# Buffers of their own for the S5 gate's sigmoid tiles, and explicit waits for each mixed piece, in a hybrid trunk kernel

## The chip, the cores and the metric

The kernel runs as one launch on one core of a Trainium2 chip. The metric is the device time of that launch in microseconds (us); lower is better. The median of three runs of the kernel before is 1204.6 us (1203.15 to 1209.52). About 0.5%, 6 us, is what a measurement can tell from no change.

## What is computed

One layer of a hybrid decoder trunk on 1024 positions of width 1024, in float32. The normalized input goes through one wide projection, whose columns feed three branches: an RG-LRU recurrence (512 wide), a gated delta rule with 8 heads of 128 (chunks of the sequence with a state carried from one to the next), and an S5 state space model (512 wide) with a gate. The three outputs stand side by side (2048 wide), are multiplied by the output weights, added to x, and a gated embedding and a last norm follow. The reference, cut to the two branches that matter here and what follows them:

```python
def step(state, inp):                      # gated delta rule, one chunk
    q_i, k_i, u_i, w_i, aqk_i, gc_i = inp
    v_new = u_i - jnp.einsum('bhcd,bhde->bhce', w_i, state)
    o_i = jnp.einsum('bhcd,bhde->bhce', q_i * jnp.exp(gc_i)[..., None], state) + jnp.einsum('bhij,bhje->bhie', aqk_i, v_new)
    state = state * jnp.exp(g_last)[..., None, None] + jnp.einsum('bhcd,bhce->bhde', k_dec, v_new)
...
z5 = jax.nn.gelu(y_s5)                     # S5 with its gate
y_s5 = z5 * jax.nn.sigmoid(z5 @ s5_w_glu[i].astype(f32) + s5_b_glu[i].astype(f32))
y_s5 = y_s5 * jax.nn.silu(s5_gate.astype(f32))
mix = jnp.concatenate([y_rg.astype(dt), y_gdn.astype(dt), y_s5.astype(dt)], axis=-1)
h = h + mix @ w_out[i]
```

## The kernel before

**How the order of the work is made.** The whole program is one Python class, `Trunk`. Its parts are generators (tasks); `spawn` (L214) registers one, a `yield` names the engine on which its next instructions are due ("pe", "v" for DVE, "a" for ACT, "g" for POOL, "d" for a DMA issue on SP), and `tick` (L248) runs those whose predecessors are done and for which there is room by a small cost model (`price`, L97; the priorities stand in `PRIO`, L57). So instructions are recorded in an order that the model decides, and `pin` (L73) holds every engine to that order. Matmuls that nothing holds up go out through `fill` (L200), which calls `tick` after every few of them: these are the filler between which the tasks' own matmuls and transposes (`mm` L195, `tr` L198) are placed. `need` (L269) keeps recording until named tasks are done.

**Precision.** Every large product is three matmuls of 128x512 in a split of float32 into a high and a low part: high times high, high times low, low times high. ACT makes the high part (a cast), DVE or POOL the low part (a subtraction).

**Stages.** A short projection of the embedding stands first; then the wide projection in 48 blocks (tiles hhi, hlo by whi, wlo into pp) is the filler for the RG-LRU, the S5 part and the heads. For each head, `k_post` multiplies the key tile kT by itself (two tiles of four 128x128 products in PSUM, 8 matmuls), DVE turns these into AT (L1130), `solve` inverts triangular blocks on DVE for two heads at once, `levels` puts the inverses together on PE, and `chain` (L1285 and after) walks 8 steps. A step of the chain is a loop through two engines: PE Sm by kT and qT (into pc, po), DVE R (L1292), PE R by XT, DVE V (L1304), PE V by kd and AQ, DVE the new Sm (L1316) and the output on (L1327). `finish` (L1345 to L1354) scales on, transposes it on PE, and stores the head to DRAM as a piece of `mix`. All heads' chains follow each other; head 7's is the last.

**The S5 gate, `glu`.** Four blocks of 128 columns; each has two halves, and each half is 12 matmuls (gzh, gzl by whi, wlo into pp), so 96 matmuls in all. ACT takes the sigmoid of a half into the tile gs (L1432), `pre` loads gz and gg and POOL multiplies them (L1412), DVE multiplies gs by the result (L1416), SP stores gs as piece 12 + i of mix (L1418). These 96 matmuls are the filler beside the chain of head 7.

**The output projection, `out_proj`.** Four groups (two halves of the columns by two halves of the rows), each over 16 pieces of mix in the order 0 to 10, 12 to 15, 11 (11 is head 7). A piece is a load from DRAM (mr, by `mstream`, L1514 to L1522), a cast on ACT and a subtraction on DVE (mhl, L1506, L1508), and 12 matmuls, so 192 a group; at most three pieces are in hand. The weights (wsr, ws) go through ACT and POOL, by `wstream`. Group 0 accumulates in the two pp and two pg buffers; pp is also what the gate's halves use.

**Slots.** SBUF is nearly full, so tiles of late stages live in slots of earlier ones (L38): kT has four, kd one, dec two, AT three, sz two, cy one. Before the change a gate tile takes slot kT for blocks 0 and 2 and slot kd for 1 and 3, so `glu` has two waits:

```python
self.need(*t[-2:-1])      # the block before the last one must be stored
if i:
    self.need(last)       # head 6 must be finished
```

`k_post` takes both of its product tiles from the pool psg, which has two buffers; the pool psa has two more.

Of the kernel before, what the change touches and what calls it, by code (L numbers as in the profile page):

```python
# [12 lines left out]
F32 = mybir.dt.float32  # L13
# [9 lines left out]
P = 128  # L23
# [5 lines left out]
HEADS = 8  # L29
# [17 lines left out]
class Trunk:  # L47
# [1051 lines left out]
    def k_post(self, h, cv):  # L1099
        nc, d = self.nc, self.hd[h]  # L1100
        kT = d["kT"]
        hs = slice(h * NT, (h + 1) * NT)
        dec = yield from self.load_dec(h)
        ss = self.tiny.tile([P, NT], F32, name="kss", bufs=2)
        AT = d["AT"] = self.slot("AT", [P, NT, P], "AT")
        yield "pe", lambda: cv[1].done and cv[1].ready <= self.now and self.room(self.psg, 2)
        pts = [self.ps(self.psg, [P, 4, P], 8) for _ in range(2)]
        for q, pt in enumerate(pts):
            if q:
                yield "pe"  # L1110
            self.products(pt, kT, kT, q)
            yield "v"
            for k in range(4):
                t = 4 * q + k
                nc.vector.scalar_tensor_tensor(out=AT[:, t, :], in0=pt[:, k, :], scalar=1.0, in1=self.ident,
                                               op0=ALU.mult, op1=ALU.mult, accum_out=ss[:, t:t + 1])
                if k == 1:
                    yield
        nc.vector.tensor_scalar(out=ss, in0=ss, scalar1=EPS, scalar2=None, op0=ALU.add)
        r = yield from self.rsqrt(self.tiny, ss, NT, "kr")  # L1120
        bp = d["bp"] = self.tiny.tile([P, NT], F32, name="bp", bufs=5)
        nc.vector.tensor_tensor(out=bp, in0=r, in1=r, op=ALU.mult)
        nc.vector.tensor_tensor(out=bp, in0=bp, in1=self.beta[:, hs], op=ALU.mult)
        sk = d["sk"] = self.tiny.tile([P, NT], F32, name="sk", bufs=5)
        nc.vector.tensor_tensor(out=sk, in0=ss, in1=r, op=ALU.mult)
        for q, pt in enumerate(pts):
            yield "v"
            for k in range(4):
                t = 4 * q + k
                nc.vector.scalar_tensor_tensor(out=AT[:, t, :], in0=pt[:, k, :], scalar=bp[:, t:t + 1],  # L1130
                                               in1=dec[:, t, :], op0=ALU.mult, op1=ALU.mult)
                if k == 1:
                    yield
        self.decs -= 1
        yield "d"
        for b in range(4):
            bs = slice(32 * b, 32 * b + 32)
            nc.sync.dma_start(out=self.adiag[h, b].rearrange("t j i -> j t i"), in_=AT[bs, :, bs])
# [261 lines left out]
            self.decs -= 1  # L1400
            zs.append((hi, lo))

    def glu(self, zs, bg):
        nc = self.nc

        def pre(i, box):
            z = self.slot("cy", [P, S], "gz")
            nc.sync.dma_start(out=z, in_=self.zd[i])
            g = self.slot("sz", [P, S], "gg")
            nc.sync.dma_start(out=g, in_=self.sgd[i])  # L1410
            yield "g"
            nc.gpsimd.tensor_tensor(out=g, in0=g, in1=z, op=ALU.mult)  # L1412
            box.append(g)

        def glu_post(i, sig, box):
            nc.vector.tensor_tensor(out=sig, in0=sig, in1=box[0].rearrange("p (j c) -> p c j", c=P), op=ALU.mult)  # L1416
            yield "d"
            nc.sync.dma_start(out=self.mix[12 + i], in_=sig.rearrange("p c j -> p (c j)"))  # L1418
        t, last = [], self.hd[HEADS - 2]["fin"]
        for i in range(4):  # L1420
            wh, wl = self.take(("g", i))
            self.need(*t[-2:-1])
            if i:
                self.need(last)
            sig = self.slot("kd" if i % 2 else "kT", [P, P, 8], "gs")
            box = []
            pr = self.spawn(pre(i, box), "d", t[-1:] + [last])
            for half in range(2):
                sl = slice(512 * half, 512 * half + 512)
                ps = self.psum()  # L1430
                self.mm3(ps, [((wh[:, k, :], wl[:, k, :]), (zs[k][0][:, sl], zs[k][1][:, sl])) for k in range(4)])
                self.drains.append(self.spawn(self.drain(ps, lambda ps, half, sl, i=i, sig=sig: nc.scalar.activation(  # L1432
                    out=sig[:, :, 4 * half:4 * half + 4].rearrange("p c j -> p j c"),
                    in_=ps.rearrange("p (j c) -> p j c", c=P), func=AF.Sigmoid, bias=bg[:, i:i + 1]), half), "a", self.drains[-1:]))
            t.append(self.spawn(glu_post(i, sig, box), "v", self.drains[-1:] + [pr]))
        return t
# [74 lines left out]
    def mstream(self):  # L1511
        nc = self.nc
        n = 0
        for nh in range(2):  # L1514
            for g in range(2):
                for k in self.korder:
                    yield "d", lambda: self.mused + 3 > n and n < len(self.ms) + 2 and (k != 4 + HEADS - 1 or self.hd[HEADS - 1]["fin"].done)
                    raw = self.slot("dec", [P, 512], "mr")
                    nc.sync.dma_start(out=raw, in_=self.mix[k, :, 512 * g:512 * g + 512])
                    m = self.slot("AT", [P, 2, 512], "mhl", F32R)  # L1520
                    self.spawn(self.split_late(raw, m, (nh, g, k), self.ms, nc.vector), "a", prio=self.PRIO["split_soon"])
                    n += 1  # L1522

    def until(self, store, key):
        self.wait(lambda: key in store)
        return store[key]
# [61 lines left out]
        self.hT[t] = (th, tlo)  # L1588

    def stream_setup(self):  # L1590
        self.ws, self.ms, self.wused, self.mused = {}, {}, 0, 0
        self.norms, self.hT, self.hs = {}, {}, {}
        self.korder = list(range(3 + HEADS)) + [12, 13, 14, 15, 3 + HEADS]

# [68 lines left out]
    def build(self):  # L1663
        tc, nc = self.tc, self.nc
        with ExitStack() as st:
# [4 lines left out]
            cp = E(tc.tile_pool(name="const", bufs=1))  # L1670
# [23 lines left out]
            with ExitStack() as s5s:  # L1694
# [17 lines left out]
                for kind, i in ORDER:  # L1712
# [11 lines left out]
                    elif kind == "x":  # L1724
                        last = rg[1:]
                        t, gate = self.rg_tile(i, rg)
# [13 lines left out]
            with tc.tile_pool(name="gdn", bufs=1) as self.gp:  # L1740
                hd = self.hd
                bg = self.load(cp, "s5_b_glu", [P, 4])
                hd[0]["solve"] = hd[1]["solve"] = self.spawn(self.solve(0), "d", [hd[0]["k"], hd[1]["k"]])
                hd[0]["levels"] = self.spawn(self.levels(0), "g", [hd[0]["solve"]])
                self.q_proj(0)
                self.v_proj(0)
                self.z_proj(0)
                zs = []
                prep = self.gdn(zs)
                hst.close()  # L1750
                self.fr = st.enter_context(tc.tile_pool(name="fr", bufs=1, side="right"))
                self.stream_setup()
                self.spawn(self.wstream(), "d", [prep])
                self.spawn(self.mstream(), "d", [prep])
                self.need(prep)
                self.glu(zs, bg)
                self.out_proj()
                self.ple(cp)


def layout(x, norm_g, w_in, rg_lambda, gdn_a_log, gdn_dt_bias, **kw):
# [38 lines left out]


def program(shapes):
    nc = bacc.Bacc("TRN2", target_bir_lowering=False, num_devices=1, dynamic_dma_scratch_size=8192)
    ins = {n: nc.dram_tensor("in_" + n, s, F32, kind="ExternalInput").ap() for n, s in shapes.items()}
    out = nc.dram_tensor("out_y", (S, D), F32, kind="ExternalOutput").ap()
    with tile.TileContext(nc) as tc:
        Trunk(tc, ins, out).build()
    nc.compile()
    return nc
# [7 lines left out]
```

## Time and profile before

| what | value |
|---|---|
| median of three runs (lowest, highest) | 1204.6 us (1203.15, 1209.52) |
| the profiled execution, its time | 1201.29 us |
| its span, first to last instruction | 1199.6 us |
| mean granted TensorE clock | 0.968 |
| PE busy | 1111.2 us (93% of the span) |
| DVE, ACT, POOL busy | 776.5, 566.2, 159.6 us (65%, 47%, 13%) |
| all DMA queues | 140.18 MB, mean 117 GB/s |

PE is the engine with the most work, and the table says how much: 88 us of the span have no matmul. An idle microsecond on PE is worth one on the end only if nothing else sets the time there, and the granted clock tells a second loss: a matmul that takes 0.40 us at the full clock takes 0.63 us when the clock is granted at half. The profiled execution is 3.3 us under the median of the runs.

### The profile page before, as it was taken

The numbers are of one execution on the slowest core, as the hardware profiler recorded it, in microseconds if no ns is written. First come the engines' busy times: TensorE is split into PE (matmuls) and PEld (weight loads), VectorE is DVE, ScalarE is ACT, GpSimd is POOL, SyncE is SP. The second block draws the span as 40 slices with busy tenths as digits, with TensorE's granted clock in tenths as the row PEclk, the third lists the DMA queues.
The fourth block names the chain that finished last, engine by engine and source line by source line (L and its number), as shares of the span: only waits on it lengthen the run. The fifth ranks groups of instructions, "written<-read, shape, count | busy, mean of one in ns | idle before, by whom it ended". The sixth has DMA issues, their size and how long they took to land. (4 is left out here: it accounts for less than half of the span.)

```text
span 1199.6 us, 17257 instructions
## 1 busy us (share of the span) xinstructions
PE 1111.2 (93%) x6165; PEld 902.7 (75%) x6165; DVE 776.5 (65%) x1933; ACT 566.2 (47%) x1138; POOL 159.6 (13%) x166
## 2 busy tenths in 40 slices
PE   6899698999979998999999999999868999999996
PEld 4576477887867776788888888878656778878885
DVE  6877586965676775886688667865744243263665
ACT  6533546745667773344534454435641243243332
POOL 1100000000001010000000000000261042044442
PEclk9999799999989999799999999999989999999999
DMA  8311345474766331212121122122454465464222
GB/s 302 114 36 44 105 126 174 109 190 101 214 198 189 101 114 32 73 47 80 54 84 53 36 93 67 53 53 81 148 187 166 129 212 175 135 202 147 71 85 92
DMA packets 85222, 140.18 MB, mean 117 GB/s; under 512 B 31760, under 2 KB 42192, under 8 KB 85136
## 3 DMA queue, kind: packets, MB, share of 16 engines
q1 hardware_dynamic: 83984, 134.88, 36.5%
q0 software_dynamic: 1152, 4.19, 0.9%
q8 instruction: 49, 0.80, 0.3%
q14 instruction: 37, 0.30, 0.1%
HBM read 97.98 MB, written 31.49 MB: 108 GB/s over the span
## 5 line engine op out<-in xcount | busy, mean ns | idle before, releaser
L195 PE MATMUL pp<-hhi,whi 128*128 128x512 f32 x768 | 315.9, 411 | 4.5 <-ACT hhi L404 2.3
L195 PE MATMUL pp<-hlo,whi 128*128 128x512 f32 x768 | 313.1, 408 | 3.1 <-DVE hlo L407 3.1
L195 PE MATMUL pp<-hhi,wlo 128*128 128x512 f32 x768 | 314.1, 409 | 1.3 <-DVE wlo L425 1.3
L195 PEld LDWEIGHTS pp<-hhi,whi 128*128 128x128 f32 x768 | 147.0, 191 | 35.6 <-ACT hhi L404 3.3
L195 PEld LDWEIGHTS pp<-hlo,whi 128*128 128x128 f32 x768 | 146.6, 191 | 33.1 <-DVE hlo L407 4.0
L195 PEld LDWEIGHTS pp<-hhi,wlo 128*128 128x128 f32 x768 | 146.5, 191 | 30.3 <-issue 2.4
L477 DVE SCALAR_TENSOR_TENSOR cy<-raw,c_gdn_conv_w,cy 128x512 f32<-128x512 f32 x144 | 108.2, 751 | 15.2 <-ACT cy L473 12.3
L1508 DVE TENSOR_TENSOR mhl<-mr,mhl 128x512 fp32r<-128x512 f32 x64 | 54.6, 854 | 88.4 <-ACT mhl L1506 88.4
L195 PE MATMUL pg<-ws,mhl 128*128 128x512 f32 x384 | 101.2, 398 | 0.5 <-ACT mhl L1506 0.5
L1508 POOL TENSOR_TENSOR ws<-wsr,ws 128x512 fp32r<-128x512 f32 x48 | 68.0, 1421 | 196.9 <-ACT ws L1506 196.7
L425 DVE TENSOR_TENSOR wlo<-wraw,whi 128x1024 fp32r<-128x1024 f32 (+1 forms) x52 | 63.1, 1214 | 40.5 <-ACT whi L423 36.9
L195 PEld LDWEIGHTS pg<-ws,mhl 128*128 128x128 f32 x384 | 71.3, 188 | 19.5 <-ACT mhl L1506 1.5
L1506 ACT CAST mhl<-mr 128x512 fp32r<-128x512 f32 x64 | 39.8, 622 | 93.5 <-DMA mr<-mix 45.0
L195 PE MATMUL pp<-ws,fth 128*128 128x512 f32 x256 | 81.3, 396 | 0.0
L487 ACT COPY raw<-pp 128x512 f32<-128x512 f32 x56 | 32.7, 584 | 84.5 <-PE pp L195 80.2
L423 ACT CAST whi<-wraw 128x1024 fp32r<-128x1024 f32 (+1 forms) x52 | 52.8, 1015 | 24.8 <-DMA wraw<-in_w_blk 24.7
L195 PEld LDWEIGHTS pp<-ws,fth 128*128 128x128 f32 x256 | 48.0, 188 | 10.9
L1330 ACT ACTIVATE osq<-on 128x128 f32<-128x128 f32 x64 | 19.7, 308 | 75.8 <-DVE on L1327 57.9
L195 PE MATMUL pp<-ws,mhl 128*128 128x512 f32 x192 | 51.2, 399 | 3.1 <-ACT mhl L1506 1.6
L1506 ACT CAST ws<-wsr 128x512 fp32r<-128x512 f32 x48 | 29.8, 622 | 47.7 <-DMA wsr<-in_w_out 28.3
L195 PE MATMUL pp<-ws,ftl 128*128 128x512 f32 x128 | 51.1, 400 | 0.0
L1304 DVE TENSOR_SCALAR V<-pc,bp 128x128 f32<-128x128 f32 x64 | 22.3, 348 | 38.1 <-PE pc L195 38.0
(414 smaller groups left out, 2033.2 us busy)
## 6 DMA issues: line engine op xcount, KB each, us to landing
wraw<-in_w_blk SPq DMA_DIRECT2D x48, 512.0 KB, 4.2
mr<-mix SPq DMA_DIRECT2D x64, 256.0 KB, 3.0
dec<-dec SPq DMA_DIRECT2D x16, 512.0 KB, 4.5
wsr<-in_w_out SPq DMA_DIRECT2D x32, 256.0 KB, 3.0
xt<-in_xT SPq DMA_DIRECT2D x16, 256.0 KB, 6.1
ppd<-po POOLq DMA_DIRECT2D x8, 512.0 KB, 4.0
gcb<-grow SPq DMA_DIRECT2D x8, 512.0 KB, 5.0
dec<-gcb SPq DMA_DIRECT2D x8, 512.0 KB, 2.8
```

The costliest lines, as they stand in the source:

```text
L195: self.nc.tensor.matmul(**kw)
L423: nc.scalar.copy(out=hi, in_=raw)
L425: nc.vector.tensor_tensor(out=lo, in0=raw, in1=hi.bitcast(F32), op=ALU.subtract)
L477: nc.vector.scalar_tensor_tensor(out=y[:, sl], in0=raw[:, j + sl.start:j + sl.stop], scalar=wconv[:, j:j + 1], in1=y[:, sl], op0=ALU.mult, ...
L487: nc.scalar.copy(out=raw[:, 3 + 512 * half:3 + 512 * half + 512], in_=ps)
L1304: v.tensor_scalar(out=V, in0=p2, scalar1=bp[:, t:t + 1], scalar2=None, op0=ALU.mult)
L1330: nc.scalar.activation(out=sq, in_=on[:, t, :], func=AF.Square, accum_out=d["so"][:, t:t + 1])
L1506: nc.scalar.copy(out=hl[:, 0, :], in_=raw)
L1508: e.tensor_tensor(out=hl[:, 1, :], in0=raw, in1=hl[:, 0, :].bitcast(F32), op=ALU.subtract)
```

## The change

1. `k_post`: heads 0 to 2 may take their two product tiles from psa when psg has no room.
2. `glu`: the tiles gs of blocks 0 to 2 come from a pool of their own, gsig, with three buffers (128 partitions by 4 KB each); only block 3 still uses the slot kd. The wait for the block before the last is gone, and the wait for head 6 stands before block 3 alone.
3. `mstream`: a piece is loaded only when what writes it is done, for every piece (function `mixed`); before, this was written for head 7 alone, since the two waits in `glu` implied the rest.
4. The SBUF scratch that the framework sets aside for DMAs issued by POOL goes from 8192 to 4096 bytes.

```diff
@@ k_post
-        yield "pe", lambda: cv[1].done and cv[1].ready <= self.now and self.room(self.psg, 2)
-        pts = [self.ps(self.psg, [P, 4, P], 8) for _ in range(2)]
+        yield "pe", lambda: cv[1].done and cv[1].ready <= self.now and (self.room(self.psg, 2) or h < 3 and self.room(self.psa, 2))
+        pool = self.psg if self.room(self.psg, 2) else self.psa
+        pts = [self.ps(pool, [P, 4, P], 8) for _ in range(2)]
@@ glu
-        t, last = [], self.hd[HEADS - 2]["fin"]
+        t, last = self.glt, self.hd[HEADS - 2]["fin"]
         for i in range(4):
             wh, wl = self.take(("g", i))
-            self.need(*t[-2:-1])
-            if i:
+            if i == 3:
                 self.need(last)
-            sig = self.slot("kd" if i % 2 else "kT", [P, P, 8], "gs")
+            sig = self.slot("kd", [P, P, 8], "gs") if i == 3 else gs.tile([P, P, 8], F32, name="gs", bufs=3)
@@ mstream
-                    yield "d", lambda: self.mused + 3 > n and n < len(self.ms) + 2 and (k != 4 + HEADS - 1 or self.hd[HEADS - 1]["fin"].done)
+                    yield "d", lambda: self.mused + 3 > n and n < len(self.ms) + 2 and self.mixed(k)
...
+    def mixed(self, k):
+        if k < 4:
+            return True
+        if k < 4 + HEADS:
+            return self.hd[k - 4]["fin"].done
+        return len(self.glt) > k - 12 and self.glt[k - 12].done
...
+                with tc.tile_pool(name="gsig", bufs=1) as gs:
+                    self.glu(zs, bg, gs)
+                    self.out_proj()
+                    self.ple(cp)
...
-    nc = bacc.Bacc("TRN2", target_bir_lowering=False, num_devices=1, dynamic_dma_scratch_size=8192)
+    nc = bacc.Bacc("TRN2", target_bir_lowering=False, num_devices=1, dynamic_dma_scratch_size=4096)
```

Since the recorded order comes from the model, these few lines move instructions in two places. The line numbers of the changed kernel are one or more higher behind `k_post`.

**First place: PE, the key products of heads 1 and 2** (kT by kT into pg; hhi and hlo by whi are filler of the wide projection). Before:

```order
L195 MATMUL pp<-hhi,wlo 128x512
L195 MATMUL pg<-kT 128x128 x4
L195 MATMUL pp<-hhi,whi 128x512
L195 MATMUL pp<-hlo,whi 128x512
L195 MATMUL pg<-kT 128x128 x4
L195 MATMUL pp<-hhi,wlo 128x512
```

Now:

```order
L195 MATMUL pp<-hhi,wlo 128x512
L195 MATMUL pg<-kT 128x128 x8
L195 MATMUL pp<-hhi,whi 128x512
L195 MATMUL pp<-hlo,whi 128x512
L195 MATMUL pp<-hhi,wlo 128x512
```

Head 1's two tiles stand together, where two filler matmuls stood between them. Head 2's two tiles, 38 and 56 filler matmuls behind head 1's last before, now stand 32 and 45 behind; the transposes of the next task's query, 108 filler matmuls behind head 1's first tile before, stand 98 behind it.

**Second place: PE, the gate beside the chain of head 7** (gzh, gzl by whi, wlo are the gate's matmuls; pg from ident,on is the finish of head 6; pc from Sm, R, V and po are the chain). Before, from the step that follows the gate's first 24 matmuls:

```order
L195 MATMUL pc<-Sm,kT 128x128
L195 MATMUL po<-Sm,qT 128x128
L198 MATMUL pg<-ident,kT 128x128
L198 MATMUL pg<-ident,on 128x128 x4
L195 MATMUL pc<-R,XT 128x128
L195 MATMUL pc<-V,kd 128x128
L195 MATMUL po<-V,AQ 128x128
L198 MATMUL pg<-ident,on 128x128 x4
L195 MATMUL pc<-Sm,kT 128x128
```

Now, around the same finish of head 6:

```order
L195 MATMUL pp<-gzh,whi 128x512
L198 MATMUL pg<-ident,on 128x128 x4
L195 MATMUL pp<-gzl,whi 128x512
L195 MATMUL pc<-R,XT 128x128
L195 MATMUL pp<-gzh,wlo 128x512
L195 MATMUL pp<-gzh,whi 128x512
L195 MATMUL pp<-gzl,whi 128x512
L195 MATMUL pp<-gzh,wlo 128x512
L195 MATMUL pp<-gzh,whi 128x512
L195 MATMUL pc<-V,kd 128x128
L195 MATMUL po<-V,AQ 128x128
L195 MATMUL pp<-gzl,whi 128x512
```

From the first of these chain steps to the next, 8 more gate matmuls stand ahead of Sm by kT, 11 between it and the finish, 9 up to the second finish and one behind that: 29 where there was none. The gate is then through at the chain's fifth step, and the matmuls of the output projection stand between those of the later steps:

```order
L195 MATMUL pp<-gzh,wlo 128x512
L195 MATMUL pp<-ws,mhl 128x512 x3
L195 MATMUL pc<-V,kd 128x128
L195 MATMUL po<-V,AQ 128x128
L195 MATMUL pp<-ws,mhl 128x512 x3
L195 MATMUL pc<-Sm,kT 128x128
L195 MATMUL po<-Sm,qT 128x128
L198 MATMUL pg<-ident,kT 128x128
L195 MATMUL pg<-ws,mhl 128x512 x6
L195 MATMUL pc<-R,XT 128x128
```

Before, the first of them stood behind the last gate matmul, which stood 18 behind the chain's end. On DVE, the product gs of block 0 moves from behind the V of a step to ahead of it; that of block 1 stays ahead of the last step's R.

**The same place on SP** (mix from gs: store of a gate block; mr: load of a piece; gz, gg: loads for the next block; wsr: output weights). Before:

```order
L1418 DMA mix<-gs 128x1024
L1408 DMA gz<-zd 128x1024
L1410 DMA gg<-sgd 128x1024
L1519 DMA mr<-mix 128x512
L1418 DMA mix<-gs 128x1024
L1519 DMA mr<-mix 128x512
```

Now:

```order
L1419 DMA mix<-gs 128x1024
L1500 DMA wsr<-in_w_out 128x512
L1409 DMA gz<-zd 128x1024
L1411 DMA gg<-sgd 128x1024
L1519 DMA mr<-mix 128x512
L1500 DMA wsr<-in_w_out 128x512
L1519 DMA mr<-mix 128x512
L1500 DMA wsr<-in_w_out 128x512
L1519 DMA mr<-mix 128x512 x2
L1419 DMA mix<-gs 128x1024
L1519 DMA mr<-mix 128x512
```

The store at the head of the first piece is that of block 1, at the head of the second that of block 0. The fourth load of a piece, the first mr here, stood behind two stores and stands behind one; four loads stand between the first two stores where there was none, four between the second and the third, three between the third and the fourth.

## Rows read from the trace of the kernel before

**Rows 1.** Busy time in stretches: PE, PEld, DVE, ACT, POOL, then PEclk, DMA share, GB/s.

```profile
335.00:500.00 165.00, 146.39 (x890) 119.81 (x890) 116.37 (x372) 100.46 (x211) 15.54 (x22) 0.92 0.38 114
...
840.00:940.00 100.00, 82.02 (x367) 65.13 (x366) 54.14 (x94) 41.08 (x82) 33.58 (x20) 0.91 0.49 166
940.00:1180.00 240.00, 239.50 (x1057) 191.92 (x1056) 116.21 (x245) 86.15 (x157) 79.63 (x59) 1.00 0.43 141
```

**Rows 2.** Waits of PE, 840 to 960 us: total us, times, longest.

```profile
PE pc L195 <- DVE R L1292: 4.8, 1, 4.8
PE pg L198 <- DVE on L1345: 4.0, 1, 4.0
PE pc L195 <- DVE Sm L1316: 2.9, 2, 2.7
PE pc L195 <- DVE V L1304: 1.7, 3, 0.8
PE pp L195 <- ACT mhl L1506: 1.6, 2, 0.8
```

**Rows 3.** PE's timeline, gate and chain: start, duration, operation, [idle before, releaser].

```profile
857.72 0.40 PE L195 MATMUL pp<-gzh,wlo 128*128 128x512 f32 x1
...
863.37 0.66 PE L198 MATMUL pg<-ident,on 128*128 128x128 f32 x4 [4.03 <-DVE on L1345]
...
899.08 0.80 PE L195 MATMUL pc<-R,XT 128*128 128x128 f32 x2 [4.77 <-DVE R L1292]
...
903.09 0.63 PE L195 MATMUL pp<-gzh,whi 128*128 128x512 f32 x1
```

**Rows 4.** PE's timeline, output projection.

```profile
908.87 0.97 PE L195 MATMUL pp<-ws,mhl 128*128 128x512 f32 x3 [0.60 <-ACT gs L1432]
...
954.91 1.56 PE L195 MATMUL pp<-ws,mhl 128*128 128x512 f32 x6
956.31 2.96 PE L195 MATMUL pg<-ws,mhl 128*128 128x512 f32 x12
```

**Rows 5.** DVE's timeline at the same places.

```profile
861.57 1.74 DVE L1345 TENSOR_TENSOR on<-on,ory 128x512 f32<-128x512 f32 x1
...
895.82 2.94 DVE L1416 TENSOR_TENSOR gs<-gs,gg 128x1024 f32<-128x1024 f32 x1 [2.52 <-POOL gg L1412]
898.69 0.34 DVE L1292 SCALAR_TENSOR_TENSOR R<-pc,negc,vn 128x128 f32<-128x128 f32 x1
...
912.98 2.01 DVE L1416 TENSOR_TENSOR gs<-gs,gg 128x1024 f32<-128x1024 f32 x1
...
925.38 2.24 DVE L1508 TENSOR_TENSOR mhl<-mr,mhl 128x512 fp32r<-128x512 f32 x2 [3.47 <-ACT mhl L1506]
```

**Rows 6.** POOL's timeline, the last block's product.

```profile
924.10 2.37 POOL L1412 TENSOR_TENSOR gg<-gg,gz 128x1024 f32<-128x1024 f32 x1 [16.62 <-DMA gg<-sgd]
```

**Rows 7.** DMA issues: queue, count, KB each, median us from issue to landing.

```profile
mr<-mix SPq DMA_DIRECT2D x64, 256.0 KB, 3.0
...
ppd<-po POOLq DMA_DIRECT2D x8, 512.0 KB, 4.0
...
gg<-sgd SPq DMA_DIRECT2D x4, 512.0 KB, 6.0
mix<-gs SPq DMA_DIRECT2D x4, 512.0 KB, 2.9
```

**Rows 8.** Waits of SP's queue, 840 to 960 us.

```profile
SPq L1418 <- DVE gs L1416: 16.2, 2, 14.1
```

**Rows 9.** Waits of PE, 325 to 500 us.

```profile
PE pg L198 <- DVE AT L1130: 2.4, 1, 2.4
PE pp L195 <- ACT sz L1214: 2.1, 1, 2.1
PE pg L195 <- DVE AT L1130: 1.2, 2, 0.9
```

**Rows 10.** POOL's own DMAs: count, min, median, max ns to issue, first and last start.

```profile
L1469 POOL DMA_DIRECT2D ppd<-po x8: 725/725/907, 15.5 to 44.7; - x8
```

More of the change, by code (lines that the diff above doesn't have):

```diff
@@ L1401, in glu_prep, with glu @@
             zs.append((hi, lo))
-    def glu(self, zs, bg):
+    def glu(self, zs, bg, gs):
         nc = self.nc
@@ L1590, in stream_setup @@
     def stream_setup(self):
-        self.ws, self.ms, self.wused, self.mused = {}, {}, 0, 0
+        self.ws, self.ms, self.wused, self.mused, self.glt = {}, {}, 0, 0, []
         self.norms, self.hT, self.hs = {}, {}, {}
@@ L1755, in build @@
                 self.need(prep)
-                self.glu(zs, bg)
-                self.out_proj()
-                self.ple(cp)
+                with tc.tile_pool(name="gsig", bufs=1) as gs:
+                    self.glu(zs, bg, gs)
+                    self.out_proj()
+                    self.ple(cp)
 def layout(x, norm_g, w_in, rg_lambda, gdn_a_log, gdn_dt_bias, **kw):
```

## The prediction

> **What bounds the kernel now.** I read three views in this order: busy time by stretch, PE's waits in the stretch with a gap, and the timelines around the longest waits. PE has most of the work, so the first view is read for where it is not busy. From 940 to 1180 us it works 239.50 of 240.00 us at the full clock, so nothing there can be gained except by starting earlier [rows 1]. From 840 to 940 us, the gate with the last chain and the start of the output projection, it works only 82.02 of 100 us: 18.0 us idle. The granted clock there is 0.91, so of the 82.02 us of work 9%, 7.4 us, are lost to the clock; a matmul that takes 0.40 us at the full clock takes 0.63 us after a long wait [rows 1, 3]. Together 25.4 us is what perfect work would save in this stretch. The third stretch that matters, 335 to 500 us, has 18.6 us idle at a clock of 0.92 [rows 1].
>
> PE's waits say what the 18.0 us are [rows 2]: 4.8 for one R, 4.0 for the scaled output of head 6, 2.9 for two Sm, 1.7 for three V, 1.6 for two pieces; the rest are below 1.1 each. All the long ones end in DVE's part of a chain step or of the finish. They are latency: PE has nothing in its queue that it may do meanwhile. In the 4.03 us wait it stood before the transposes of head 6 although 72 gate matmuls were still to come [rows 3], since they were recorded only after that finish. DVE was not fast either: the scaling took 1.74 us and R stood behind a product gs of 2.94 us [rows 5].
>
> **The gate's buffers and the wait for head 6 (parts 2 and 3).** Nothing is added to any engine's work: the same 96 and 192 matmuls, sigmoids, products, stores and loads. What moves is the filler. One matmul is worth 1.40/6 = 0.233 us at the full clock, from two neighbours six apart [rows 4].
>
> The first wait: 19 more gate matmuls now stand ahead of the first transposes (8 and 11), 19 x 0.233 = 4.4 us against 4.03 idle [rows 3]: it goes, and with it the slow clock behind it. Ten more follow until the next step. The chain itself is not faster: its steps hang on PE and DVE in turn, as before. By the fifth step the gate is through, some 29 matmuls (6.8 us) ahead of its old place relative to the chain; from there the output projection fills, 59 matmuls (13.8 us) until the last step's R, where 4.8 and most of 2.9 were waited [rows 2].
>
> What stays: (a) three short waits for V or R behind something long on DVE; the product of block 0 now stands ahead of a V, and three like waits cost 1.7 [rows 2]; I leave 1.7. (b) The output projection's first tiles need pp, which the last sigmoids hold; the like wait was 0.60 [rows 4], and if the sigmoid stands on ACT behind a cast whose load has yet to land it is up to one load more, 3.0 [rows 7]: between 0.60 and 3.6 I take 1.9, since casts of weights and the sigmoids alternate there. (c) The last gate block's piece can be loaded only after its store: 2.9 + 3.0 [rows 7] and, as an estimate, 1.6 for issue and split, 7.5 in all, against about 20 matmuls in hand, 4.7: 2.8 remain; ends 0, and 7.5 if nothing is in hand. Sum 6.4. Of the clock's 7.4 us, which came behind three waits of 2.7 to 4.8, I keep a third, 2.5, for the one wait of that size that is left; ends 0 and 5.
>
> So this stretch gains 25.4 - 6.4 - 2.5 = 16.5 us; ends: 23.1 (b 0.6, c 0, no dip) and 7.6 (b 3.6, c 7.5, clock 5).
>
> **The loads' order on SP (part 3).** The explicit waits add no instruction. SP's queue is in order, and behind a store of a gate block wait the loads of pieces. Before, one store held the queue 14.1 us for its product [rows 8], and the fourth piece stood behind two stores. Now it stands behind one, with four, four and three loads between the later stores: four pieces are 48 x 0.233 = 11.2 us of PE work. A block's loop from store to store is load 6.0, POOL 2.37, DVE 2.01 to 2.94 and some 0.3 of issue, about 11.2 [rows 5 to 7]. These are equal, so I cost it at nothing beyond (c); the cover is gone if the loop grows, which is the second and fifth case below.
>
> **DVE beside POOL.** The pieces' splits on DVE now run while POOL still works for gate and weights. Two splits that met POOL's product took 2.24 us together [rows 5, 6]; a product gs beside weight splits took 2.94 against 2.01 alone [rows 5]. The sum takes 0.9 for such a meeting, hidden by pieces in hand. The Trainium skill (SBUF — State Buffer, "SBUF: two separate sides") says that an operation on two SBUF inputs and a GpSimd one that reads SBUF exclude each other for the whole of an instruction. The 0.9 agrees in direction, and no row shows the whole of POOL's 2.37 paid on a path.
>
> **The key products (part 1).** Head 1's two waits, 1.2 us, go: its second tile no longer waits for AT of the first to leave PSUM. The query's transposes waited 2.4 for AT; they now stand 10 matmuls (2.3 us) earlier, but so do head 2's products, 6 and 11 matmuls (1.4 and 2.6 us): I take 1.1. The wait for sz, 2.1, stays [rows 9]. Behind this comes the chain of head 0, which waits for the inverses; these need AT of heads 0 and 1, which is earlier. Gain 2.3. Ends: 5.7 (all three rows of the group), and -2.4, the same longest wait once more, if psa's buffers or the shifted order on DVE make a later task wait.
>
> **The scratch (part 4).** POOL issues eight DMAs, 15.5 to 44.7 us [rows 10]. Were each held until the one before had landed, 8 x 4.0 = 32.0 against these 29.2 [rows 7, 10]: at most 2.8 us, on POOL, beside PE's work at the start. No row suggests a gain. I take 0.
>
> **Sum.** 16.5 + 2.3 = 18.8. The profiled execution takes 1201.29, so 1182.5; it lies 3.3 under the median, which I add: **1185.8 us**. Its own range by the ends above is 1176 (23.1 + 5.7) to 1199 (7.6 - 2.4). Bound for faster and slower: 0.5%, 6 us.
>
> **The rivals.**
> *SP gives part of it back* (0.15). If the block loop takes the 14.1 us that a store once waited [rows 8], each of three loops outlasts four pieces by 2.9: 8.7, less the 2.8 already counted, with a clock dip of 2.5: 1185.8 + 8.4 = 1194. For it: the queue is in order. Against: the 14.1 came with a chain step's R and V between.
> *The chain bounds it* (0.12). All long waits end in the chain's or finish's DVE steps [rows 2]; if gate and output matmuls only change places among these and PE waits as long elsewhere, only the key products count: 1204.6 - 2.3 = 1202. This is also the case in which freeing the slots does not do what it is there for. Against: 88 matmuls of filler that stood behind the chain now stand in it.
> *DVE and POOL exclude each other* (0.05). If each of three gate products on POOL holds a piece's split for its whole 2.37 rather than 0.9, on the path [rows 5, 6]: 3 x 1.5 = 4.4, so 1190. The skill's rule above would bring this.
> *Slower* (0.05). The place is the load of gg between two stores. POOL once waited 16.62 for it [rows 6]. If that recurs, a loop is 16.62 + 2.37 + 2.94 = 21.9, 10.7 more than four pieces feed, three times 32, less 2.8: 1215. It decides from a loop of some 19.5: three times (19.5 - 11.2) eats the gain and 6 more. Against: that wait fell behind the store that held SP for 14.1.
>
> **How the numbers follow.** The forecast has 0.63; it, the skill's case and SP's are faster by over 0.5%: 0.83. The chain's case is same, 0.12; slower 0.05. The range leaves out the last two, 0.17: 1176 to 1199, the forecast's own ends, with SP's and the skill's case inside.
>
> **What would show it.** In the changed profile, 840 to 940 us: PE busy above 90 of 100 us, a clock of 0.95 or more; the wait for the scaled output of head 6 gone; the last R's 4.8 gone; the first group of the output projection ending some 17 us earlier. At the key products the 1.2 us gone. It is wrong if PE waits for pieces (mhl) by more than 6 us in that stretch, if SP's wait for gs stays above 14, or if the stretch from 335 to 500 us has more idle time than before.

## The result, and the profile after

The changed kernel takes 1190.12 us (median of four, 1188.19 to 1193.25) against 1206.46 (1203.15 to 1209.52) in the same session: ratio 0.987, interval 0.983 to 0.991. Run again beside three experiments it took 1189.37, ratio 0.984 (0.981 to 0.987). That is 16 to 18 us faster; forecast were 18.8.

The profiled execution, however, spans 1191.5 us against 1199.6 of before: 8.1 us, half of that. So the first thing to read is where in the program the two traces part. Four marks stand in PE's timeline of every kernel here: the first key product of head 0, the first matmul of head 0's chain (pc from vn, XT), the first gate matmul (pp from gzh), and the first matmul of the output projection's second group (pc from ws). The stretches between them, in us, each the difference of two starts:

```
kernel                      to the first   keys to     chain 0    gate to     to the
                            key product    chain 0     to gate    2nd group   end
before                         333.7         123.3       394.0      108.1      240.5
changed                        340.8         123.1       394.8       92.3      240.6
changed, again                 338.5         122.1       393.3       94.2      240.6
```

The gate stretch lost 14 to 16 us. The rest is the first column: 7.1 us more up to the first key product, where both programs have the same instructions in the same order. Whether that belongs to the change or to the one execution is a question for the experiments. How much a single profile can say is read from the profiles of all the kernels below: with the old gate (three kernels) the gate stretch took 108.1, 108.4 and 108.8 us, with the new one (three profiles) 92.3, 93.5 and 94.2. From the first key product to chain 0 the thirteen profiles lie between 119.5 and 124.7, and from the second group to the end, where all kernels do the same work, between 238.9 and 242.3.

The waits of PE from 840 to 960 us in the changed kernel (columns as in [rows 2]) show what is left of the 18.0 us:

```profile
PE pp L195 <- ACT mhl L1506: 2.6, 1, 2.6
PE pp L195 <- ACT gs L1432: 1.5, 1, 1.5
PE pc L195 <- DVE V L1305: 1.4, 3, 0.9
PE pp L195 <- DVE mhl L1508: 1.2, 3, 0.6
PE pg L198 <- DVE on L1346: 0.5, 1, 0.5
PE pc L195 <- ACT kd L1299: 0.5, 1, 0.5
PE po L195 <- DVE on L1328: 0.2, 1, 0.2
```

Sum 7.9. The 4.8 for R and the 2.9 for Sm have no successor; the scaled output of head 6 fell from 4.0 to 0.5; one wait of 2.6 for a piece is new. The busy times of the same stretches (columns as in [rows 1]):

```profile
335.00:500.00 165.00, 148.56 (x892) 122.44 (x891) 120.80 (x368) 105.49 (x223) 16.05 (x24) 0.91 0.39 119
840.00:940.00 100.00, 94.02 (x463) 75.25 (x461) 60.17 (x106) 46.12 (x92) 33.21 (x20) 1.00 0.53 177
940.00:960.00 20.00, 17.97 (x69) 14.14 (x70) 8.47 (x11) 5.53 (x9) 2.61 (x2) 0.91 0.60 189
```

From 840 to 940 us PE is busy 94.02 where it was 82.02, with 463 matmuls where there were 367, and the clock is never below full. The one dip left in this profile, 0.91, stands in the 20 us behind the new wait. PE's timeline there (start, duration, operation, [idle before, releaser]):

```profile
937.89 1.56 PE L195 MATMUL pg<-ws,mhl 128*128 128x512 f32 x6
942.03 1.96 PE L195 MATMUL pp<-ws,mhl 128*128 128x512 f32 x6 [2.58 <-ACT mhl L1506]
943.80 2.75 PE L195 MATMUL pg<-ws,mhl 128*128 128x512 f32 x6
```

Six matmuls that take 1.56 before the wait take up to 2.75 behind it. What the wait is for stands in SP's queue: the stores of the four gate blocks.

```profile
892.68 0.42 SPq L1419 DMA_DIRECT2D mix<-gs  x1
909.48 0.32 SPq L1419 DMA_DIRECT2D mix<-gs  x1
923.38 0.32 SPq L1419 DMA_DIRECT2D mix<-gs  x1
928.48 0.32 SPq L1355 DMA_DIRECT2D mix<-sz  x1
935.97 0.32 SPq L1419 DMA_DIRECT2D mix<-gs  x1
```

The last store is issued at 935.97, and PE goes on at 942.03, 6.1 us later: store, load and split of the last gate piece. Head 7's piece (mix from sz) was stored 7.5 us ahead of it, though it comes behind it in the projection.

At the key products (waits of PE from 325 to 500 us, as in [rows 9]) the 1.2 us are gone, and others have grown:

```profile
PE pg L195 <- DVE s_X L1028: 5.2, 1, 5.2
PE pg L198 <- DVE AT L1131: 3.3, 1, 3.3
PE pc L195 <- DVE V L1305: 2.7, 5, 0.5
PE pp L195 <- ACT raw L487: 2.0, 2, 1.2
PE pg L195 <- DVE Xs L1234: 1.5, 2, 0.8
```

### The profile page after: what moved, and what is told of

It reads as the page before. It is cut to its first block, busy times and chain, and to the rows that moved or that the text cites. A ratio compares the mean times of both kernels' runs of the same rounds, so it can differ in the third digit from the quotient of the medians.

```text
span 1191.5 us, 17246 instructions
## 1 busy us (share of the span) xinstructions
PE 1112.1 (93%) x6165; PEld 903.9 (76%) x6165; DVE 784.9 (66%) x1933; ACT 565.7 (47%) x1138; POOL 158.8 (13%) x166
## 5 line engine op out<-in xcount | busy, mean ns | idle before, releaser
L1508 DVE TENSOR_TENSOR mhl<-mr,mhl 128x512 fp32r<-128x512 f32 x64 | 61.5, 963 | 76.4 <-ACT mhl L1506 76.3
L1506 ACT CAST mhl<-mr 128x512 fp32r<-128x512 f32 x64 | 39.8, 621 | 77.3 <-DMA mr<-mix 45.6
L195 PEld LDWEIGHTS pp<-ws,fth 128*128 128x128 f32 x256 | 48.0, 188 | 10.9
L195 PEld LDWEIGHTS pp<-ws,mhl 128*128 128x128 f32 x192 | 35.5, 190 | 15.5 <-ACT mhl L1506 3.0
```

The lines of the kernel that those rows point to most:

```text
L195: self.nc.tensor.matmul(**kw)
L1506: nc.scalar.copy(out=hl[:, 0, :], in_=raw)
L1508: e.tensor_tensor(out=hl[:, 1, :], in0=raw, in1=hl[:, 0, :].bitcast(F32), op=ALU.subtract)
```

## The experiments

**The parts apart, and the start.** Three kernels and the change itself ran on one chip. The first has part 1 alone:

```diff
 # k_post, on the kernel before
-        yield "pe", lambda: cv[1].done and cv[1].ready <= self.now and self.room(self.psg, 2)
-        pts = [self.ps(self.psg, [P, 4, P], 8) for _ in range(2)]
+        yield "pe", lambda: cv[1].done and cv[1].ready <= self.now and (self.room(self.psg, 2) or h < 3 and self.room(self.psa, 2))
+        pool = self.psg if self.room(self.psg, 2) else self.psa
+        pts = [self.ps(pool, [P, 4, P], 8) for _ in range(2)]
```

> The kernel before with part 1 alone (the key products of heads 0 to 2 may take the other PSUM pool). Theory, after the changed profile: from the first key product to the first step of head 0's chain the changed kernel took 123.1 us against 123.3, so the two waits that went (1.2 us) came back before that chain, and this kernel is within 1 us of the kernel before. Rival (the prediction's step): part 1 is worth 2.3 us, so 0.2% faster. Second rival: its other order on DVE costs something that only the gate's gain hid, and it is slower by 1 us or more.

Measured: 1207.26 us against 1207.11 of the kernel before, ratio 1.000 (0.998 to 1.002); from the keys to chain 0 it took 124.7 us. The medians fit the theory, but the interval reaches from 2.5 us faster to 2.9 slower, so it leaves room for the 2.3 us of the first rival too: the part is worth no more than that, and these runs cannot say more.

The second is the change without that part.

```diff
 # k_post, on the changed kernel
-        yield "pe", lambda: cv[1].done and cv[1].ready <= self.now and (self.room(self.psg, 2) or h < 3 and self.room(self.psa, 2))
-        pool = self.psg if self.room(self.psg, 2) else self.psa
-        pts = [self.ps(pool, [P, 4, P], 8) for _ in range(2)]
+        yield "pe", lambda: cv[1].done and cv[1].ready <= self.now and self.room(self.psg, 2)
+        pts = [self.ps(self.psg, [P, 4, P], 8) for _ in range(2)]
```

> The changed kernel without part 1: own buffers for the gate, the moved wait for head 6, explicit waits for pieces, small scratch. Theory: all of the gain is here, 15 to 17 us under the kernel before and within 1 us of the whole change; from the first gate matmul to the first matmul of the output projection's second group it takes some 92 us, against 108.1 before and 92.3 with the whole change. Rival: part 1 carries 2.3 us of the gain, so this is some 14 us faster and 2.3 slower than the whole change.

Measured: 1189.62 us, ratio 0.983 (0.979 to 0.987), beside 1189.37 for the whole change. The gate stretch is 93.5 us. As far as these runs can tell, all of the gain is in the gate.

The third changes the scratch alone, on the kernel before.

```diff
-    nc = bacc.Bacc("TRN2", target_bir_lowering=False, num_devices=1, dynamic_dma_scratch_size=8192)
+    nc = bacc.Bacc("TRN2", target_bir_lowering=False, num_devices=1, dynamic_dma_scratch_size=4096)
```

> The kernel before with the scratch for POOL's DMAs at 4096 bytes, nothing else; every instruction stands where it stood. In the changed profile the first key product came 7.1 us later than before (340.8 against 333.7), though the instructions up to there are the same. Theory: that is from one execution to the next (the clock in the first 335 us), not the scratch: no difference in the median, within 3 us, and the first key product anywhere from 333 to 342. Rival: the scratch slows the start by some 7 us, so 1213 against 1206, and the first key product stands near 341 again.

Measured: 1206.68 us, ratio 0.999 (0.997 to 1.002); the first key product at 337.8. And the change once more:

> The whole change once more, beside the three others on one chip. Theory: 15 to 17 us under the kernel before; the gate stretch again 92 us, while the start (to the first key product) may come out anywhere from 333 to 342 us. Rival (the scratch slows the start): the first key product again at 341 and every kernel with the small scratch like it.

Measured: 1189.37 us; first key product at 338.5. Over all profiles of this study that mark lies between 333.7 and 341.9 us, in kernels that have the same instructions up to there, with the large scratch (333.7 and 335.5) and the small one (336.4 to 341.9). The two groups do not overlap, with only two profiles in the first, so the marks alone do not settle it; the timed runs of the third kernel do to 2 us, since the upper end of its interval is 1.0015. The 7.1 us of the first table are not the scratch's; most of them is the spread between executions.

**Which of the two waits in the gate mattered.** The change takes away two: for head 6, and for the block before the last. Each was put back alone, with the tiles keeping their own buffers.

```diff
             wh, wl = self.take(("g", i))
-            if i == 3:
+            if i:
                 self.need(last)
```

> The whole change, but blocks 1 and 2 of the gate wait for the finish of head 6 as before (the tiles keep buffers of their own, the wait for the block before the last is gone). In the order the 8 gate matmuls ahead of the next chain step, the 11 ahead of head 6's transposes and the 10 behind are gone again; gate matmuls fill the later steps, and the output projection still starts before the chain ends. Theory: the moved wait is worth the 4.0 us idle ahead of those transposes and the slow clock behind it, some 7 us together: gate stretch 99 us against 92 to 94, so about 1196 against 1189. Rival: the buffers do all of it, and the time stays at 1189. Second rival: the wait does all of it, and the time goes back to 1205 to 1207.

Measured: 1193.47 us, ratio 0.988 (0.983 to 0.992), gate stretch 95.1 us. Between theory and rival: 1 to 3 us of the stretch, not 7. Yet both losses are there in full. PE's waits from 845 to 965 us, and the stretch behind the first of them (columns as above):

```profile
PE pg L198 <- DVE on L1346: 4.2, 2, 4.0
PE pp L195 <- ACT gs L1432: 2.0, 1, 2.0
...
860.00:880.00 20.00, 14.80 (x70) 12.65 (x69) 10.42 (x24) 11.04 (x24) 8.59 (x8) 0.74 0.58 193
```

The 4.0 is back, and the clock falls to 0.74. But the wait of 2.6 for the last gate piece is not among this kernel's waits. PE is later, and the piece is also earlier: its store is issued 73.6 us behind the first gate matmul, against 77.3 and 78.1 in the two profiles of the change and 78.6 in the kernel before. The four products and stores follow each other one by one, since `pre` loads a block's gz and gg only when the block before is stored and head 6 is finished, so the gate's matmuls, put earlier on PE, did not bring the last store forward by more than about 1 us. In the change its first round is longer, 16.8 us from store to store against 14.3, and most of this stands on DVE. POOL has the product gg of block 1 ready at 904.16, but two splits of pieces are ahead of block 1's gs, each longer than the 0.69 of one alone, as POOL works beside them:

```profile
902.93 1.79 DVE L1508 TENSOR_TENSOR mhl<-mr,mhl 128x512 fp32r<-128x512 f32 x1 [1.78 <-ACT mhl L1506]
904.64 0.33 DVE L1317 SCALAR_TENSOR_TENSOR Sm<-Sm,egl,pc 128x128 f32<-128x128 f32 x1
904.90 1.52 DVE L1508 TENSOR_TENSOR mhl<-mr,mhl 128x512 fp32r<-128x512 f32 x1
906.34 0.28 DVE L1328 TENSOR_TENSOR on<-oi,po 128x128 f32<-128x128 f32 x1
906.54 2.91 DVE L1417 TENSOR_TENSOR gs<-gs,gg 128x1024 f32<-128x1024 f32 x1
```

In the fourth experiment no split stands there, and gs starts at 899.16, 0.03 us behind gg. So what was won at the start of the stretch was partly paid again at its end.

```diff
             wh, wl = self.take(("g", i))
+            self.need(*t[-2:-1])
             if i == 3:
```

> The whole change, but each gate block from 2 on again waits until the block before the last is stored (the wait for head 6 stays at block 3 alone, the buffers stay). In the order, chain steps 2 to 5 of head 7 then have no gate matmul between them, and all of the output projection stands behind the chain. Theory: with nothing between, a chain step leaves PE idle for 2 us or more and the clock falls, so about all of the gain goes: gate stretch 105 to 110 us, 1202 to 1207 in all. Rival: what was won is the start of the stretch alone (the wait at head 6), which stays here: some 7 us of the gain remain, about 1199.

Measured: 1205.34 us, ratio 0.999 (0.996 to 1.001), gate stretch 108.3 us: as the theory said, all of the gain is gone as far as the interval tells (4.6 us faster to 1.1 slower). With nothing between the steps, PE's waits and the stretch of these steps read:

```profile
PE pc L195 <- DVE R L1293: 5.6, 2, 3.0
PE pg L198 <- DVE on L1346: 3.2, 3, 2.3
PE pp L195 <- ACT mhl L1507: 2.9, 1, 2.9
...
880.00:900.00 20.00, 15.86 (x57) 12.64 (x56) 7.24 (x15) 7.95 (x23) 10.31 (x6) 0.55 0.65 215
```

57 matmuls in 20 us at a clock of 0.55, where the change does 91 at 1.00:

```profile
880.00:900.00 20.00, 17.19 (x91) 13.75 (x90) 7.31 (x15) 11.05 (x26) 11.91 (x8) 1.00 0.64 210
```

The buffers, by the wait for a stored block that they make needless, carry the change.

**The new wait at the end.** The last two pieces of the projection were exchanged:

```diff
-        self.korder = list(range(3 + HEADS)) + [12, 13, 14, 15, 3 + HEADS]
+        self.korder = list(range(3 + HEADS)) + [12, 13, 14, 3 + HEADS, 15]
```

> The whole change with the last two pieces of the output projection exchanged: head 7's piece (11) before the last gate block's piece (15). PE's order stays the same. Theory: the 2.6 us that PE waits for the last gate piece is its store's and load's time with nothing left to do, so 12 matmuls (2.8 us) more in front hide it, and with it the granted clock of 0.91 behind it (1.8 us of 20): gate stretch 4 us shorter, about 89, and 4 us (0.35%) under the whole change. Rival: head 7's own piece is as late (its store stands 7.5 us ahead of the gate's), PE waits for that one instead, and nothing changes.

Measured: 1184.85 us, ratio 0.982 (0.978 to 0.985), gate stretch 89.0 us. Run again:

> The exchange of the last two pieces once more, beside the two kernels built on it, on one chip. Gate stretch 89 us, 1183 to 1187 in all; 3 to 5 us under the whole change.

Measured: 1187.29 us, ratio 0.983 (0.981 to 0.986), stretch 89.2. So 3 to 5 us of the stretch in both profiles (92.3 and 94.2 in the change), and 2 to 5 in the medians, whose intervals overlap. PE's waits in the first of the two:

```profile
PE pc L195 <- DVE V L1305: 1.6, 3, 0.9
PE pp L195 <- ACT gs L1432: 1.5, 1, 1.5
PE pp L195 <- DVE mhl L1508: 1.3, 2, 0.7
PE pp L195 <- ACT mhl L1506: 0.7, 1, 0.7
...
940.00:960.00 20.00, 19.76 (x85) 15.65 (x84) 8.36 (x11) 7.39 (x12) 6.68 (x5) 1.00 0.71 228
```

2.6 has become 0.7, and the clock of 0.91 is 1.00. The theory holds.

With this at hand the question of the fourth experiment could be put again: what is the wait for head 6 worth when the end of the stretch no longer takes it back? The edit is the one shown there, on the kernel with the exchange.

> The kernel with the last two pieces exchanged, and in it blocks 1 and 2 of the gate wait for the finish of head 6 as before. Without the exchange that wait cost only 1 to 3 us of the gate stretch (95.1 us against 92.3 to 94.2), although PE stood for 4.0 us and the clock fell to 0.74 behind it; but there PE no longer waited 2.6 us for the last gate piece. Theory: the last gate piece's store and load set the end of the stretch in the whole change, so starting the gate earlier was mostly given back there; with that piece last, the wait for head 6 costs its full 5 to 7 us: gate stretch 94 to 96 us against 89.0 with the exchange alone, so 1190 to 1192 against 1185. Rival: the wait costs 2 us whatever stands at the end (the filler that it takes away is used up later anyway): 91 us, 1187.

Measured: 1193.97 us, ratio 0.989 (0.986 to 0.992), gate stretch 95.7 us against 89.0 and 89.2. The theory holds: 6.5 us, where it was 1 to 3 with the old order of pieces. The medians, each as a ratio to the kernel before in its own session, say the same: 7 to 9 us here, 1 to 4 with the old order. The two losses at the start, 4.0 idle and 20 us at a clock of 0.74, are the same as there. One more dip, 0.91 from 900 to 920 us, stands in this profile alone; it is up to 1.8 of the 6.5 us, and what it comes from is not shown.

**Two attempts at what is left.** The product of the sigmoid tile was cut in two, with the exchange in place:

```diff
-            nc.vector.tensor_tensor(out=sig, in0=sig, in1=box[0].rearrange("p (j c) -> p c j", c=P), op=ALU.mult)
+            gg = box[0].rearrange("p (j c) -> p c j", c=P)
+            for c in (slice(0, 64), slice(64, P)):
+                if c.start:
+                    yield "v"
+                nc.vector.tensor_tensor(out=sig[:, c, :], in0=sig[:, c, :], in1=gg[:, c, :], op=ALU.mult)
```

> The kernel with the last two pieces exchanged, and in it the product of the sigmoid tile cut into two halves on DVE, so that the V of a chain step stands between the halves of block 0. Theory: PE's wait for that V (0.9 us) goes down to 0.3 or less, the output projection starts somewhat earlier, and the total is 0.5 to 1 us under the kernel without the cut, which no median here can tell. Rival: the halves each wait for POOL's work on the port that they share, each costs 1.5 rather than 1.0 us, and the wait for V stays.

Measured: 1187.14 us, ratio 0.983 (0.980 to 0.987), gate stretch 90.0. Nothing won. DVE's and POOL's timelines show why:

```profile
881.91 2.16 DVE L1421 TENSOR_TENSOR gs<-gs,gg 128x512 f32<-128x512 f32 x1 [1.82 <-POOL gg L1413]
883.99 0.34 DVE L1305 TENSOR_SCALAR V<-pc,bp 128x128 f32<-128x128 f32 x1
884.25 1.86 DVE L1421 TENSOR_TENSOR gs<-gs,gg 128x512 f32<-128x512 f32 x1
...
881.83 3.38 POOL L1512 TENSOR_TENSOR ws<-wsr,ws 128x512 fp32r<-128x512 f32 x2
```

A half takes 1.07 to 1.08 us alone and 2.16 here, so V still waits for most of a whole product. PE's wait for it went from 0.9 to 0.64, not to 0.3. The rival was right in kind for this block: each of its halves paid for POOL (1.08 and 0.78 us).

The other one lets the projection's first tiles be those that the gate does not use:

```diff
-        sets = [[(self.psp, "pp")] * 2 + [(self.psg, "pg")] * 2,
+        sets = [[(self.psg, "pg")] * 2 + [(self.psp, "pp")] * 2,
```

> The kernel with the last two pieces exchanged, and in it the first and third group of the output projection use the two pg buffers for their first two row tiles and the two pp buffers for the others. The tile that waited 1.5 us for the gate's last sigmoid is then written 6 matmuls (1.4 us) later. Theory: that wait goes to 0.3 or less and nothing takes its place: gate stretch 87.5 us against 89.0, 1 to 1.5 us under. Rival: the chain of head 7 and the gate's last piece set the end, the wait only moves to a later piece or chain step, and the stretch stays at 89.

Measured: 1184.24 us, ratio 0.982 (0.979 to 0.985), gate stretch 88.7. PE's waits:

```profile
PE pg L195 <- DVE mhl L1508: 2.0, 3, 0.9
PE pc L195 <- DVE V L1305: 1.7, 2, 1.3
PE pg L195 <- ACT mhl L1506: 0.9, 1, 0.9
```

The wait for the sigmoid is gone, but those for DVE's splits (by 0.5 to 0.6), for V (0.1 to 0.3) and for ACT's casts (0.2) are longer than in the two profiles with the exchange alone, and the stretch is 0.3 to 0.5 shorter, less than one profile can tell. The rival fits the trace; the median, 3 us lower, cannot be told from its base. The three kernels with the exchange and without the wait for head 6 are the fastest of the study, and the runs do not tell them apart.

Not tried: fewer than three own buffers, a second slot for gz, so that a block's loads need not wait for the store before, and loads of pieces without the explicit waits, which belong to the order that the buffers make possible.

## Why the prediction was right, and where it was not

The time came out 4.3 us above the forecast and in the range; the mechanism was the one forecast. The gate fell short by 0.7 to 2.6 us, the key products by some 1, the offset by some 2. Of the signs named ahead, PE's 94.02 us, the clock of 1.00 and the missing 4.8 came as said; the wait for head 6's output is 0.5 and not gone. The three signs of being wrong stayed away: 3.8 us of waits for pieces, 5.8 for SP's longest wait for gs, 16.4 us idle from 335 to 500 us against 18.6. Step by step:

**The gate.** Forecast were 16.5 us from 25.4 less what stays; the stretch shrank by 13.9 to 15.8 (from 108.1 to 94.2 and 92.3). The four terms of what stays, in the order of the prediction: short waits for V 1.7, measured 1.4; the sigmoid in the way of the projection's first tile 1.9, measured 1.5; the last gate piece 2.8, measured 2.6; the clock 2.5, measured 1.8 (9% of the 20 us behind that wait). What the list lacked are 1.2 for DVE's splits and some 1.2 in three smaller waits. In the second profile of the change the same terms read 0.9, 2.3, 2.7 and, for the clock, some 3.4 (0.94 and 0.89 in two stretches of 20 us), and 1.9 for the splits: the sum is met better than its terms. The second term was where it was said to be. ACT's timeline of the changed kernel:

```profile
891.84 0.62 ACT L1506 CAST ws<-wsr 128x512 fp32r<-128x512 f32 x1 [2.31 <-DMA wsr<-in_w_out]
892.36 1.20 ACT L1432 ACTIVATE gs<-pp,c_s_b_glu 128x512 f32<-128x512 f32 x1
```

ACT stood 2.31 us for a weight's load with the sigmoid behind it, while PE had ended the half that it reads at 889.7.

**The key products: the term that was too large.** "I take 1.1" of the transposes' wait of 2.4, and 2.3 us in all. The two waits of 1.2 went, as forecast. But the transposes, 10 filler matmuls earlier, waited longer, 3.3 and not 1.3 (3.2 or 3.3 in all ten profiles with part 1): AT came when DVE had done it, so what was won ahead of it was waited there. The wait for sz, 2.1, which was to stay, is no longer listed; 2.0 for ACT's copies (raw) stand in its place, 0.9 in most of the other profiles, and the one for Xs grew from 0.7 to 1.5. The stretch from the first key product to chain 0, before and in the two profiles of the change (columns as in [rows 1]):

```profile
333.68:456.99 123.31, 110.63 (x633) 91.48 (x632) 86.56 (x249) 87.28 (x167) 15.54 (x22) 0.96 0.47 143
340.78:463.88 123.10, 110.59 (x633) 92.14 (x632) 89.45 (x249) 87.20 (x167) 14.74 (x22) 0.96 0.47 143
338.47:460.57 122.10, 110.62 (x633) 91.77 (x632) 89.54 (x249) 87.08 (x167) 14.22 (x22) 0.96 0.48 144
```

PE is idle for 12.7 us before, 12.5 in the first and 11.5 in the second. Over all profiles it is 12.7 to 12.9 in the three kernels without part 1 and 10.9 to 12.5, mean 11.5, in the ten profiles with it: some 1.3 us less waiting, where 2.3 were forecast. That this shortens the whole is not shown; the kernel with this part alone measured 1.000 (0.998 to 1.002). The lower end of the term, -2.4, was not reached either.

**The order of loads on SP.** It was costed at nothing beyond the last piece, since a block's loop and four pieces both took 11.2 us. The loops took longer: 16.8, 13.9 and 12.6 us between the stores above. The trace of before already had 15.2, 16.3 and 14.5 there; the sum of durations left out what stands between them, such as 1.7 to 2.1 us from the store to the load of gg and the two splits ahead of block 1's gs. PE nevertheless waited only 3.8 us in all for pieces (2.6 and 1.2). The estimate of the loop was wrong and its consequence small; that the chain's steps and the gate's remaining matmuls, which also stand between, and the three pieces in hand covered it is an argument, not shown. So the condition of the rival in which SP gives part back, a loop of 14.1, came true (14.4 in the mean of the three), and its price of 8.4 did not: what was given back was one place, the last piece.

**The scratch.** Taken as 0, measured 0.999.

**Adding the terms.** The prediction let the first wait's 4.0 us and its clock go in full and the last piece's wait come as a term of its own. The waits for head 6 put back without and with the exchange show that these are not independent: the former is worth 6.5 us with the last piece out of the way and 1 to 3 with it. The sum was near since both were in it.

**The rivals.** That the chain bounds the stretch whatever is put between is refuted by the change and shown in its pure form by the fifth experiment, whose 108.3 is the stretch of before. The case in which the three gate products on POOL each hold a split for their whole 2.37 did not come: PE waited 1.2 for DVE's splits, three times, and the splits that met POOL's work lost 0.8 to 1.1 each, as the 0.9 of the forecast; they were not only hidden, though, but delayed block 1's gs. Nor did the slower one: POOL waited 10.85 us for the last gg, and PE not at all for it beyond the last piece.

**The offset.** 3.3 us were added from the profiled execution to the median. The median of before in later sessions is 1206.3 to 1207.1, and the start of that execution, 333.7 us, was the shortest of all here; the offset was some 2 us too small.

## What to carry to other kernels

When an engine waits in a latency chain, look for what keeps independent work from being recorded between its steps: here it was a tile's slot that was free only after a store, and three buffers of 4 KB a partition were worth some 1.5%. Before adding up waits that will go, ask which transfer ends last at the end of the stretch, since it takes back what is won ahead of it; moving that transfer's consumer to the last place shortened the stretch by 3 to 5 us more. And compare stretches between marks that both programs have, not spans, when executions of one program differ by as much as the change.

## What was not expected of the hardware

The stretch up to the first key product took 333.7 to 341.9 us over the profiles, in kernels with the same instructions there; the granted clock in it was 0.96 in the profile of before and 0.95 in the changed one's, with dips in other places. One profiled execution thus says nothing on a few us in the whole. The stretch from the second group of the projection to the end, the same work in all of them, is steadier: 238.9 to 242.3.

DVE beside POOL could be read more exactly than the prediction did. The first half product above starts 0.08 us behind a POOL subtraction, which alone takes 1.27 to 1.30, and takes 1.08 longer than alone; the whole product in the changed kernel, 3.06 against 2.01, starts 0.08 us behind one as well and is 1.05 longer:

```profile
888.07 3.06 DVE L1417 TENSOR_TENSOR gs<-gs,gg 128x1024 f32<-128x1024 f32 x1 [1.82 <-POOL gg L1413]
887.99 4.28 POOL L1508 TENSOR_TENSOR ws<-wsr,ws 128x512 fp32r<-128x512 f32 x2
```

The Trainium skill (SBUF — State Buffer, "SBUF: two separate sides") says that whichever of the two starts first has the shared port pair for its whole instruction and the other one blocks. These rows agree with it: what DVE loses, 1.05 and 1.08, is close to the 1.2 that is left of the POOL instruction when it starts.
